# A hybrid S5, retention and ConvGLU layer on one Trainium2 core: S5 state tables for chunks of 16 steps in place of 8, with the side work paced anew

## The chip, the core and the metric

The kernel runs on one core of a Trainium2 chip. The time is the device time of one execution in microseconds (us). A core has five engines with queues of their own: PE (TensorE, matrix products; PEld is its weight load), DVE (VectorE), ACT (ScalarE), POOL (GpSimd) and SP (SyncE, which here issues the transfers). They meet only at semaphores.

## The reference, cut to what matters

```python
hx = modulate(rms_norm(x, norm1_w), mx[0], mx[1])              # 2048 tokens x 1024, 256 context tokens likewise
ux, qx, kx, vx, gx = split_projection(hx @ w_in, rotate=True)  # S5 input u (512), retention q, k, v, g (512 each)
# S5: 32 groups x 16 channels, complex diagonal state of 64, both directions
bu = einsum('gnp,blgp->blgn', b_bar, u);  h[t] = lam_bar * h[t-1] + bu[t]
y  = real(einsum('gpn,blgn->blgp', c_mat, h_f + h_b)) + d * u
s5_x = gelu(y) * sigmoid(gelu(y) @ w_glu + b_glu)
# retention: 4 heads of 128, chunks of 128 tokens, both directions, per-head norm, swish gate
ret_x = retention_mixer(qx, kx, vx, gx, ...)
x = x + mx[2] * (concat([s5_x, ret_x]) @ w_out)
x = x + mx[5] * conv_ffn(modulate(rms_norm(x, norm2_w), mx[3], mx[4]), w_up, conv_w, conv_b, w_down)
return rms_norm(x, final_norm_w)
```
`mx` are the six adaLN vectors, `silu(c) @ w_mod + b_mod`. All data are float32.

## The kernel before, in words

**Stages.** (1) Table stage, 0 to 264 us: adaLN for the first norm, norm and transposition of the tokens in tiles of 256 (`norm_tile`, L563), the S5 input projection (`u_tile`, L615), the S5 tables (`s5_tables`, L422) and the retention's context state. (2) Sweeps, 264 to 897 us. (3) GLU stage, 897 to about 1010 us. (4) Output projection, to 1210. (5) The up half of the FFN, to 2112. (6) The down half, to 2618. Stages 4 to 6 hold no line of the change.

Large products are made of three float32r matmuls (`mm3`, L153 to L156: high by high, high by low, low by high); smaller ones (S5, retention) are plain float32, and the trace shows each of those as two records. Splits into high and low are an ACT copy and a subtraction at L159.

**S5.** The state is not advanced token by token. Tables let one matmul inject 8 tokens of a group into a chunk state (`Dinj`, from JT and JO), one read 8 outputs from the state before a chunk (`Drd`, from GT), and one add what the tokens of a chunk give each other (the Toeplitz table `DT`, from TT). So 2304 tokens (256 context, 2048 latent) are 288 chunks, held as 18 blocks of 16. `s5_tables` makes the tables in 8 groups of four steps: GT (six DVE operations, L433 to L438), TT (PE L450, DVE L456 to L460, a store), JT (six POOL operations, L470 to L475), JO (PE transposes L482, ACT L484, a store L485). One step is taken per round of the norm and projection loop, the rest before the context tile.

**S5 generator** (`s5_gen`). For each of 4 batches of 8 groups: `s5_inj` loads U and the tables and injects (PE L887, ACT L889 to L891 into X); `s5_scan` runs 15 steps within the blocks, all 18 blocks abreast (four DVE operations on 128x288, L904 to L907), then 17 steps over the blocks (four on 128x16, L916 to L919); `s5_fix` carries the block states in (DVE L933 to L939, POOL L932 to L940, on 128x480, 16 rounds in all); `s5_read` copies X to E (ACT L956, L957), multiplies (PE L965 to L967), applies GELU and stores (L970).

**Sweeps.** Sixteen sweeps (two halves of the tokens, four heads, first k and v, then q and g) of eight units; a unit is 24 float32r matmuls of 256 columns, rotary work on DVE (L802, L803), POOL (L804) and copies on ACT. The loop that drives them counts a ninth unit for each k-v sweep, so two sweeps are 17 units and all are 136. Side work is stepped from that loop: the S5 generator at 1.9 steps per unit until it ends; then, after two units, the retention generators (`ret_gen`, one per head, put on a list when the q-g sweep of the second half of their head is done) at two steps per unit; and, from sweep 9, the late modulation (`mod_late`: 16 pieces, each a 1 MB load, eight DVE operations at L685 and L687, one PE matmul L691, three steps a piece). What is left of the retention is stepped four at a time in the rounds of the GLU stage (`glu_gen`).

The instruction order of each engine is made when the program is built, by a scheduler that follows program order, priorities and its own timeline.

## Time and profile before

| what | value |
|---|---|
| median of 3 runs (lowest, highest) | 2618.12 us (2611.74, 2619.86) |
| the profiled execution: its own time, its span | 2620.0 us, 2618.2 us |
| PE, PEld busy | 92%, 78% of the span |
| DVE, ACT, POOL busy | 65%, 39%, 45% |
| mean granted TensorE clock | 0.973 |

The shares are means over six stages with different limits; for this change only the first three count. Busy time of an engine is the time in which at least one of its instructions ran, and an instruction that waits for a port counts as running. PE's ends are modelled, so its work is better counted in matmuls times the distance between their starts.

### The profile page before, as it was taken

The numbers are of one execution on the slowest core, as the hardware profiler recorded it, in microseconds if no ns is written. First come the engines' busy times: TensorE is split into PE (matmuls) and PEld (weight loads), VectorE is DVE, ScalarE is ACT, GpSimd is POOL, SyncE is SP. The second block draws the span as 40 slices with busy tenths as digits, with TensorE's granted clock in tenths as the row PEclk, the third lists the DMA queues.
The fourth block names the chain that finished last, engine by engine and source line by source line (L and its number), as shares of the span: only waits on it lengthen the run. The fifth ranks groups of instructions, "written<-read, shape, count | busy, mean of one in ns | idle before, by whom it ended". The sixth has DMA issues, their size and how long they took to land.

```text
span 2618.2 us, 35766 instructions
## 1 busy us (share of the span) xinstructions
PE 2421.5 (92%) x12896; PEld 2039.7 (78%) x12896; DVE 1700.4 (65%) x3387; ACT 1009.7 (39%) x1697; POOL 1189.6 (45%) x852
## 2 busy tenths in 40 slices
PE   7889987888899978997999999999999999999998
PEld 3779887777898967885788888778888878788876
DVE  9893398998386695667656656756556543636454
ACT  2444746563432442222333333433333332324332
POOL 2354253454334352212677777877777700303120
PEclk9899999999999989999999999999999999999999
DMA  8545633435787653556222222422222264545442
GB/s 251 194 144 144 165 97 108 123 120 177 226 250 246 213 182 123 157 167 198 103 97 73 73 97 73 153 73 75 93 76 75 75 253 145 198 144 197 156 169 89
DMA packets 334319, 377.83 MB, mean 144 GB/s; under 512 B 43942, under 2 KB 284410, under 8 KB 331838
## 3 DMA queue, kind: packets, MB, share of 16 engines
q1 hardware_dynamic: 332702, 374.98, 44.5%
q8 instruction: 102, 1.67, 0.3%
q10 hardware_dynamic: 1440, 0.56, 0.1%
q14 instruction: 75, 0.61, 0.1%
HBM read 268.00 MB, written 107.47 MB: 143 GB/s over the span
## 4 chain that ended last, share of the span: by engine, by line
PE 59%; DVE 20%; DMA 7%; ACT 4%; issue 4%; POOL 3%; SPq 2%; DVEq 0%; ACTq 0%; POOLq 0%
PE mm L1504 17%; PE sc L1504 9%; PE y L1504 4%; PE mm L154 4%; PE mm L155 4%; PE mm L156 4%; PE y L154 2%; PE y L155 2%; PE y L156 2%; POOL w L159 2%; PE sc L154 2%; PE sc L155 2%; PE sc L156 2%; DMA x<-in_x_dram 1%; PE tr L154 1%
## 5 line engine op out<-in xcount | busy, mean ns | idle before, releaser
L159 POOL TENSOR_TENSOR w<-stg,w 128x512 fp32r<-128x512 f32 (+1 forms) x268 | 538.3, 2024 | 214.2 <-ACT w L1440 95.1
L1504 PE MATMUL mm<-hc,w 128*128 128x512 f32 x2112 | 526.1, 397 | 11.3 <-POOL w L159 7.4
L1504 PEld LDWEIGHTS mm<-hc,w 128*128 128x128 f32 x2112 | 398.1, 189 | 111.1 <-POOL w L159 9.2
L1504 PE MATMUL sc<-hc,w 128*128 128x512 f32 x1056 | 278.1, 399 | 2.3 <-POOL w L159 1.4
L159 DVE TENSOR_TENSOR bw<-draw,bw 128x1536 fp32r<-128x1536 f32 x88 | 159.1, 1813 | 183.8 <-ACT bw L1622 183.5
L1504 PEld LDWEIGHTS sc<-hc,w 128*128 128x128 f32 x1056 | 200.3, 190 | 52.4 <-POOL w L159 2.4
L1622 ACT ACTIVATE bw<-draw 128x1536 fp32r<-128x1536 f32 x88 | 130.6, 1487 | 270.5 <-PE tr L156 214.7
L804 POOL TENSOR_TENSOR ob<-ra,rb 128x128 f32<-128x128 f32 x128 | 72.8, 569 | 311.0 <-DVE rb L803 192.6
L154 PE MATMUL mm<-w,hT 128*128 128x256 f32 x688 | 207.5, 302 | 1.9 <-ACT ob L849 1.9
L155 PE MATMUL mm<-w,hT 128*128 128x256 f32 x688 | 204.9, 298 | 0.0
L156 PE MATMUL mm<-w,hT 128*128 128x256 f32 x688 | 204.3, 297 | 0.0
L1649 POOL TENSOR_TENSOR acc<-acc,tm 128x512 f32<-128x512 f32 x24 | 35.1, 1484 | 325.9 <-DVE tm L1648 318.3
L1504 PE MATMUL y<-hc,w 128*128 128x512 f32 x528 | 150.3, 396 | 0.0
L154 PEld LDWEIGHTS mm<-w,hT 128*128 128x128 f32 x688 | 134.6, 196 | 6.6 <-ACT ob L849 2.4
L155 PEld LDWEIGHTS mm<-w,hT 128*128 128x128 f32 x688 | 134.3, 195 | 2.3 <-issue 0.4
L156 PEld LDWEIGHTS mm<-w,hT 128*128 128x128 f32 x688 | 133.8, 194 | 2.1 <-issue 0.4
L1597 DVE TENSOR_TENSOR A<-A,t 128x1024 f32<-128x1024 f32 x44 | 78.3, 1780 | 77.0 <-ACT A L1515 40.8
L1504 PEld LDWEIGHTS y<-hc,w 128*128 128x128 f32 x528 | 99.1, 188 | 24.0
L1429 ACT ACTIVATE w<-stg 128x512 fp32r<-128x512 f32 x44 | 27.8, 633 | 213.5 <-POOL stg L1427 213.5
L155 PE MATMUL y<-w,hT 128*128 128x256 f32 x336 | 102.8, 306 | 0.0
L156 PE MATMUL y<-w,hT 128*128 128x256 f32 x336 | 102.3, 304 | 0.0
L159 POOL TENSOR_TENSOR mh<-mix,mh 128x1024 fp32r<-128x1024 f32 x16 | 38.9, 2431 | 138.9 <-ACT mh L1338 114.4
(464 smaller groups left out, 6397.9 us busy)
## 6 DMA issues: line engine op xcount, KB each, us to landing
stg<-in_w_up_dram SPq DMA_DIRECT2D x44, 1024.0 KB
draw<-in_w_down_dram SPq DMA_DIRECT2D x88, 512.0 KB
stg<-in_w_in_dram SPq DMA_DIRECT2D x44, 512.0 KB
Dact<-A SPq DMA_DIRECT2D x44, 512.0 KB
draw<-Dact SPq DMA_DIRECT2D x88, 256.0 KB
stg<-in_w_mod_dram SPq DMA_DIRECT2D x16, 1024.0 KB
hst<-Dhc SPq DMA_DIRECT2D x10, 1024.0 KB
wm<-in_w_mod_dram SPq DMA_DIRECT2D x8, 1024.0 KB
```

The costliest lines, as they stand in the source:

```text
L154: PE.matmul(ps, lh, rh, start=start, stop=False)
L155: PE.matmul(ps, lh, rl, start=False, stop=False)
L156: PE.matmul(ps, ll, rh, start=False, stop=stop)
L159: eng.tensor_tensor(lo, src, hi.bitcast(F32), op=ALU.subtract)
L804: (GP if 1 else V).tensor_tensor(dst.rearrange("p (i j) -> p i j", j=2), ta, tb, op=ALU.add)
L1429: A.activation(w[:, 0, j], x, AF.Copy)
L1504: PE.matmul(ps, wt[:, wl, j, k], t[:, tl, k], start=start and k == 0 and m == 0, stop=k == 3 and m == 2, skip_group_check=not start)
L1597: V.tensor_tensor(As[j], As[j], T1[j], op=ALU.mult)
L1622: A.activation(w[:, 0], s, AF.Copy)
L1649: (V if g == NG - 1 else GP).tensor_tensor(ac[:, ns], ac[:, ns], tm, op=ALU.add)
```

## The change

A chunk becomes 16 steps. U stays in the old layout of 8 and is read with a step of 2, so each product over a chunk is two matmuls, for the even and the odd half. There are 144 chunks, 9 blocks of 16. The tables GT (10 powers to 18), TT (15 to 31), JT and JO (8 to 16) about double; TT and JO now share one buffer, JO is made and stored in two halves. `s5_fix` takes four groups at a time in two rounds per batch. The late modulation starts with sweep 3, and the retention takes 2.34 steps per unit. The h tiles get 96 bytes more per partition.

```diff
-        return h_pool.tile([P, 2, KT, TS], F32R, tag="hT", name="hT", bufs=4)
+        return h_pool.tile([P, 2 * KT * TS + 24], F32R, tag="hT", name="hT", bufs=4)[:, 0:2 * KT * TS].rearrange("p (l k n) -> p l k n", l=2, k=KT)
...
-    V.tensor_copy(pw[:, 9], pw[:, 8])
+    cmul_pow(pw, 9, 8, 1, 8)
+    V.tensor_copy(pw[:, 17], pw[:, 16])
...
-            GT = s_pool.tile([P, 2, 4, 10, Q], F32, tag="GT", name="GT")
+            GT = s_pool.tile([P, 2, 4, 18, Q], F32, tag="GT", name="GT")
...
-            V.tensor_tensor(GT[:, 1], GT[:, 1], tA, op=ALU.subtract)
+            V.scalar_tensor_tensor(GT[:, 1], GT[:, 1], -1.0, tA, op0=ALU.mult, op1=ALU.subtract)
...
-            TT = s_pool.tile([64, 2, 15, Q], F32, tag="TT", name="TT")
+            TT = s_pool.tile([64, 2, 31, Q], F32, tag="JO", name="TT")
...
-            V.tensor_copy(TT[:, :, 0:7], pv1[:, :, 0:7])
-            V.tensor_copy(TT[:, :, 8:15], pv0[:, :, 1:8])
+            V.tensor_copy(TT[:, :, 0:15], pv1[:, :, 0:15])
+            V.tensor_copy(TT[:, :, 16:31], pv0[:, :, 1:16])
...
-            JT = s_pool.tile([P, 2, 4, T8, Q], F32, tag="JT", name="JT")
+            JT = s_pool.tile([P, 2, 4, T16, Q], F32, tag="JT", name="JT")
...
-            JO = s_pool.tile([P, 4, 2, P], F32, tag="JO", name="JO")
             for g2 in range(2):
-                pj = ps_sc()
+                JO = s_pool.tile([P, 2, 4, P], F32, tag="JO", name="JO")
                 for j in range(2):
+                    pj = ps_sc()
                     for r in range(2):
-                        PE.transpose(pj[:, (2 * j + r) * P:(2 * j + r + 1) * P],
-                                     JT[:, r, 2 * g2 + j].rearrange("p s q -> p (s q)"), ident)
-                A.activation(JO[:, 2 * g2:2 * g2 + 2].rearrange("p g r c -> p (g r c)"), pj, AF.Copy)
-            SP.dma_start(Dinj[b][:, hb * 1024:(hb + 1) * 1024], JO.rearrange("p g r c -> p (g r c)"))
+                        for h in range(2):
+                            PE.transpose(pj[:, (2 * r + h) * P:(2 * r + h + 1) * P],
+                                         JT[:, r, 2 * g2 + j, 8 * h:8 * h + 8].rearrange("p s q -> p (s q)"), ident)
+                    A.activation(JO[:, j].rearrange("p a c -> p (a c)"), pj, AF.Copy)
+                SP.dma_start(Dinj[b][:, (2 * hb + g2) * 1024:(2 * hb + g2 + 1) * 1024], JO.rearrange("p g a c -> p (g a c)"))
...
                 for r in range(2):
-                    ps = next(alt_s) if wide[0] else ps_sc()
-                    PE.matmul(ps[:, 0:NCC], mt[:, gi, r], Us[-1][:, g % 4], start=True, stop=True)
+                    for h in range(2):
+                        PE.matmul(ps[:, r * MCC:(r + 1) * MCC], mt[:, gi, r, h], Uh[:, h], start=(h == 0), stop=(h == 1))
...
+                A.activation(Xg[0:64, :, 0:KB], blk(pv[0:64]), AF.Copy)
+                A.activation(Xg[64:128, :, 0:1], blk(pv[64:128, :, 0:MCX][:, :, ::-1]), AF.Copy)
+                A.activation(Xg[64:128, :, 1:KB], blk(pv[64:128, :, MCX:MCC][:, :, ::-1]), AF.Copy)
...
-            pa = s_pool2.tile([P, GB, 2, 18], F32, tag="fa", name="pa")
+            pa = s_pool2.tile([P, GB, 2, KB], F32, tag="fa", name="pa")
...
-        for k in range(1, 18):
+        for k in range(1, KB):
...
-        for g4 in range(4):
-            go = 2 * g4
+        for g4 in range(2):
+            go = 4 * g4
...
-            M = s_pool2.tile([P, 4, P], F32, tag="M", name="M", bufs=1)
+            M = s_pool2.tile([P, 4, 3, P], F32, tag="M", name="M", bufs=1)
...
-                    PE.matmul(ps[:, 0:NCL], M[:, g], Us[g4][:, g, NCX:NCC], start=True, stop=False)
-                    PE.matmul(ps[:, 0:NCL], rd[:, 0, gi], Ev[:, gi, 0], start=False, stop=False)
-                    PE.matmul(ps[:, 0:NCL], rd[:, 1, gi], Ev[:, gi, 1], start=False, stop=True)
+                    PE.matmul(pv, M[:, g, 1], Uh, start=True, stop=False)
+                    for h in range(2):
+                        PE.matmul(pv[:, h], M[:, g, 2 * h], Uh[:, 1 - h], start=False, stop=False)
+                        PE.matmul(pv[:, h], rd[:, 0, gi, h * P:(h + 1) * P], Ev[:, gi, 0], start=False, stop=False)
+                        PE.matmul(pv[:, h], rd[:, 1, gi, h * P:(h + 1) * P], Ev[:, gi, 1], start=False, stop=h == 1)
...
                 with tc.high_priority(offset=1):
-                    ok = not pend or step(pend[0], 2)
+                    racc += 2.34
+                    n = int(racc)
+                    racc -= n
+                    ok = not pend or step(pend[0], n)
...
-            if i >= 9 and ucount % 1 == 0:
+            if i >= 3:
                 step(ml)
```

## Rows read from the trace of the kernel before

**Rows 1.** Busy time by stage; columns: stretch, length, engines busy, clock, DMA share, GB/s
```profile
64.00:210.00 146.00, 123.82 (x970) 109.15 (x970) 130.53 (x272) 68.68 (x126) 65.98 (x48) 0.94 0.53 164
264.00:345.00 81.00, 75.36 (x521) 69.56 (x520) 41.01 (x111) 57.73 (x144) 20.13 (x23) 0.98 0.54 149
345.00:690.00 345.00, 286.16 (x1886) 262.34 (x1887) 295.78 (x740) 187.48 (x348) 164.80 (x147) 0.95 0.45 131
690.00:897.00 207.00, 194.49 (x1535) 184.32 (x1534) 135.36 (x527) 64.50 (x185) 75.53 (x101) 0.98 0.76 237
897.00:1032.00 135.00, 103.68 (x731) 96.01 (x730) 111.24 (x314) 58.63 (x116) 55.15 (x45) 0.89 0.55 174
```

**Rows 2.** Timeline of PE: start, duration, records; three places
```profile
885.74 0.28 PE L154 MATMUL mm<-w,hT 128*128 128x256 f32 x1
...
886.92 0.28 PE L155 MATMUL mm<-w,hT 128*128 128x256 f32 x1
...
373.68 0.59 PE L967 MATMUL sc<-E,rd 128*128 128x256 f32 x2
374.11 0.59 PE L966 MATMUL tr<-E,rd 128*128 128x256 f32 x2
...
208.02 0.93 PE L482 MATMUL sc<-cst,JT 128*128 128x128 f32 x7
```

**Rows 3.** Groups of instructions, DVE, 0 to 264 us: count | busy, mean ns | idle
```profile
L435 DVE TENSOR_TENSOR GT<-GT,ct 128x640 f32<-128x640 f32 x8 | 6.5, 810 | 0.0
...
L457 DVE COPY TT<-sc 64x224 f32<-64x224 f32 x8 | 3.0, 374 | 0.0
```

**Rows 4.** Groups of instructions, POOL, 64 to 210 us, then 264 to 697 us
```profile
L475 POOL TENSOR_TENSOR JT<-JT,ct 128x512 f32<-128x512 f32 x8 | 11.4, 1430 | 0.6
...
L935 POOL TENSOR_TENSOR X<-X,fb 128x480 f32<-128x480 f32 x16 | 22.6, 1411 | 0.9
```

**Rows 5.** Timeline of DVE while POOL makes one JT: start, duration
```profile
166.97 1.03 DVE L165 TENSOR_SCALAR rsy<-vv 128x2 int32<-128x2 int32 x1
...
168.64 1.02 DVE L173 TENSOR_TENSOR rst<-rsy 128x2 f32<-128x2 f32 x1
...
170.33 1.24 DVE L174 SCALAR_TENSOR_TENSOR rst<-rst,vv 128x2 f32<-128x2 f32 x1
171.60 0.16 DVE L175 SCALAR_TENSOR_TENSOR rsy<-rst,rsy 128x2 f32<-128x2 f32 x1
```

**Rows 6.** Timeline of POOL in the same stretch
```profile
167.93 1.72 POOL L473 TENSOR_TENSOR JT<-PJ,BB 128x512 f32<-128x512 f32 x1
```

**Rows 7.** Groups of instructions, DVE, 264 to 697 us
```profile
L906 DVE TENSOR_TENSOR X<-X,pa 128x288 f32<-128x288 f32 x60 | 37.1, 619 | 0.1
...
L687 DVE SCALAR_TENSOR_TENSOR mac<-stg,sil,mac 128x256 f32<-128x256 f32 x38 | 25.5, 672 | 0.6
L918 DVE TENSOR_TENSOR X<-X,qa 128x16 f32<-128x16 f32 x68 | 19.6, 288 | 0.0
...
L939 DVE TENSOR_TENSOR X<-X,fa 128x480 f32<-128x480 f32 x16 | 18.1, 1133 | 0.3
```

**Rows 8.** Groups of instructions, ACT, 264 to 697 us
```profile
L956 ACT ACTIVATE E<-X 64x1088 f32<-64x1088 f32 x16 | 35.0, 2186 | 8.3 <-PE tr L967 4.5 <-POOL X L940 3.7
...
L889 ACT ACTIVATE X<-tr 64x288 f32<-64x288 f32 x32 | 21.4, 669 | 1.6 <-PE tr L887 1.1
```

**Rows 9.** Groups of instructions, PE, 690 to 897 us
```profile
L155 PE MATMUL mm<-w,hT 128*128 128x256 f32 x349 | 103.1, 295 | 0.0
```

**Rows 10.** The two stores that end the S5 and the GLU: ns, first and last start in us
```profile
L970 SPq DMA_DIRECT2D Dy<-Y x128: 302/422/1327, 376.6 to 696.6; - x128
...
L1234 SPq DMA_DIRECT2D Ds<-so x32: 319/320/627, 907.5 to 1009.9; - x32
```

**Rows 11.** Busy time of the stretch after the last piece of late modulation, columns as in Rows 1
```profile
860.00:890.00 30.00, 30.00 (x255) 29.84 (x254) 12.36 (x56) 9.92 (x26) 12.24 (x17) 1.00 0.54 160
```

**Rows 12.** Instructions of tile mac: ns min/median/max, first and last start in us
```profile
L691 PE MATMUL sc<-mac,cst x32: 377/377/634, 643.5 to 857.1; 128*1 128x256 f32 x32
```

More of the change, by code (lines that the diff above doesn't have):

```diff
@@ L31 @@
 NCC = NCL + NCX
+T16 = 16
+MCL = SEQ // T16
+MCX = CTX // T16
+MCC = MCL + MCX
+KB = MCC // 16
+KP = 10
 GB = 8
@@ L104, in layer_kernel @@
     Du = dram("Du", [512, T8, NCC])
-    DT = dram("DT", [G // 2, 33, 480])
-    Dinj = dram("Dinj", [NB, P, GB * 2 * P])
-    Drd = dram("Drd", [NB, P, 2 * GB * P])
+    DT = dram("DT", [G // 2, 33, 992])
+    Dinj = dram("Dinj", [NB, P, GB * 4 * P])
+    Drd = dram("Drd", [NB, P, 2 * GB * 2 * P])
     Dtab = dram("Dtab", [P, 34 * G])
@@ L228, in load_x @@
         SP.dma_start(XT[t], xsrc[t])
-    lam = s_pool.tile([G, 2, P], F32, name="lam")
-    stp = s_pool.tile([G, 2], F32, name="stp")
+    lams = s_pool.tile([G, 2 * P + 2], F32, tag="ct2", name="lam")
+    lam = lams[:, 0:2 * P].rearrange("g (r n) -> g r n", r=2)
+    stp = lams[:, 2 * P:2 * P + 2]
     for d, nm in enumerate(("f", "b")):
@@ L298, in late_columns @@
         V.tensor_copy(dcol, pt[0:64, 0:8])
-    sw = [s_pool.tile([G, P], F32, name=f"sw{i}") for i in range(6)]
+    sws = s_pool.tile([G, 8, P], F32, tag="JO", name="sw")
+    sw = [sws[:, i] for i in range(6)]
     exp_to(n_pool, stp, stp, G, 2)
@@ L372, in layer_kernel @@
     V.tensor_tensor(BB[:, 1], BB[:, 1], t1v, op=ALU.add)
[L374 to L375 removed]
+    ptab = s_pool.tile([P, 18 * 2 * G + 17 * 2 * G], F32, tag="JT", name="ptab")
+    pw = ptab[:, 0:1152].rearrange("p (e r g) -> p e r g", e=18, r=2)
     V.memset(pw[:, 0, 0], 1.0)
@@ L884, in s5_inj @@
                 g = 2 * g4 + gi
+                ps = next(alt_s) if wide[0] else ps_sc()
+                Uh = Us[-1][:, g % 4].rearrange("p (c h) -> p h c", h=2)
                 for r in range(2):
-                    ps = next(alt_s) if wide[0] else ps_sc()
-                    PE.matmul(ps[:, 0:NCC], mt[:, gi, r], Us[-1][:, g % 4], start=True, stop=True)
-                    Xg = X[:, g, r].rearrange("p (j k) -> p k j", k=18)
-                    A.activation(Xg[0:64], ps[0:64, 0:NCC].rearrange("p (k j) -> p k j", j=16), AF.Copy)
-                    A.activation(Xg[64:128, 0:2], ps[64:128, 0:NCX][:, ::-1].rearrange("p (k j) -> p k j", j=16), AF.Copy)
-                    A.activation(Xg[64:128, 2:18], ps[64:128, NCX:NCC][:, ::-1].rearrange("p (k j) -> p k j", j=16), AF.Copy)
+                    for h in range(2):
+                        PE.matmul(ps[:, r * MCC:(r + 1) * MCC], mt[:, gi, r, h], Uh[:, h], start=(h == 0), stop=(h == 1))
+                pv = ps[:, 0:2 * MCC].rearrange("p (r c) -> p r c", r=2)
+                Xg = X[:, g].rearrange("p r (j k) -> p r k j", k=KP)
+                blk = lambda v: v.rearrange("p r (k j) -> p r k j", j=16)
+                A.activation(Xg[0:64, :, 0:KB], blk(pv[0:64]), AF.Copy)
+                A.activation(Xg[64:128, :, 0:1], blk(pv[64:128, :, 0:MCX][:, :, ::-1]), AF.Copy)
+                A.activation(Xg[64:128, :, 1:KB], blk(pv[64:128, :, MCX:MCC][:, :, ::-1]), AF.Copy)
                 yield
     def s5_scan(b, X, lb):
-        Xk = X.rearrange("p g r (j k) -> p g r k j", k=18)
-        lr = lb[:, :, 0:1].unsqueeze(3).to_broadcast([P, GB, 2, 18])
+        Xk = X.rearrange("p g r (j k) -> p g r k j", k=KP)[:, :, :, 0:KB]
+        lr = lb[:, :, 0:1].unsqueeze(3).to_broadcast([P, GB, 2, KB])
         li = s_pool2.tile([P, GB, 2], F32, tag="li", name="li", bufs=2)
@@ L923, in s5_fix @@
     def s5_fix(b, X, lb, E):
-        Xk = X.rearrange("p g r (j k) -> p g r j k", k=18)
-        for g4 in range(4):
-            go = 2 * g4
-            S = lambda r: Xk[:, go:go + 2, r, 15:16, 1:17].to_broadcast([P, 2, 15, 16])
-            Lp = lambda r: lb[:, go:go + 2, 17 * r:17 * r + 15].unsqueeze(3).to_broadcast([P, 2, 15, 16])
-            o = lambda r: Xk[:, go:go + 2, r, 0:15, 2:18]
-            fa = s_pool2.tile([P, 2, 15, 16], F32, tag="fa", name="fa")
-            fb = s_pool2.tile([P, 2, 15, 16], F32, tag="fb", name="fb")
+        Xk = X.rearrange("p g r (j k) -> p g r j k", k=KP)
+        NK = KB - 1
+        for g4 in range(2):
+            go = 4 * g4
+            sh = [P, 4, 15, NK]
+            S = lambda r: Xk[:, go:go + 4, r, 15:16, 0:NK].to_broadcast(sh)
+            Lp = lambda r: lb[:, go:go + 4, 17 * r:17 * r + 15].unsqueeze(3).to_broadcast(sh)
+            o = lambda r: Xk[:, go:go + 4, r, 0:15, 1:KB]
+            fa = s_pool2.tile(sh, F32, tag="fa", name="fa")
+            fb = s_pool2.tile(sh, F32, tag="fb", name="fb")
             GP.tensor_tensor(fb, Lp(0), S(1), op=ALU.mult)
@@ L1152, in layer_kernel @@
     acc = 0.0
+    racc = 0.0
     ucount = 0
```

85 lines of the change are left out of this document (41 added, 44 removed).

## The prediction, made before the changed kernel ran

> **What bounds the kernel now.** I read the page's slices first, then the busy time by stage, then the groups and timelines inside the stages that the change touches. The busy time by stage [rows 1] shows two stages in which DVE, not PE, is full: the table stage, where DVE is busy for 130.5 of 146 us, and the sweeps that carry the S5 generator, 295.8 of 345 us. Behind them, from 690 to 897 us, PE is the fuller one (194.5 of 207, DVE 135.4), and in the GLU stretch DVE leads again (111.2 of 135 against 103.7).
>
> PE's real work is better counted in matmuls. Ten float32r matmuls of 256 columns start within 1.18 us, so one takes 0.118 and a unit of 24 takes 2.83 us; two float32 records of 256 columns take 0.43 us; the seven transposes of 128 columns, 0.93 us with a 0.27 us tail, stand 0.11 apart [rows 2]. With these, 690 to 897 us holds 349 x 3 matmuls of a sweep [rows 9] (123.5 us), and its other 488 records (42 of state updates and 26 of modulation at 0.215, 420 at 0.11) 61 us: 184 us of work in 207, a share of 0.89. The S5 part, 264 to 690, holds 83 units (235 us), 86 state records (18), 128 injection records of 288 columns (31) and 192 read records (41): 327 of 426 us, a share of 0.77. After the last modulation piece, whose matmul is at 857 [rows 12], PE is full for 30 of 30 us [rows 11].
>
> DVE's busy time contains waiting. While POOL makes one JT, a DVE operation on 128x2 takes 1.02 or 1.24 us, and one of the same kind takes 0.16 us once POOL's operation has ended [rows 5, 6]. In the 4.6 us from 166.97 to 171.60, all covered by POOL, DVE did five operations (two of 0.8 us, three small ones) worth about 2 us: each microsecond of POOL cost DVE about half a microsecond.
>
> **The table stage (loss).** GT: 48 operations go from 640 to 1152 elements. A 640-element operation takes 810 ns [rows 3], an undisturbed 288-element one 0.46, so an element costs 1.0 ns and each operation 0.52 us more: +25 us. TT: 16 copies of 224 elements, 374 ns [rows 3], become 480: 0.26 us each, +4. The larger power tables in the set-up, six products of 256 elements and eight copies longer by 256, less one operation dropped: +4. Together +33 us of DVE's own time. The subtraction turned into a three-operand form I price at nothing, being one operation for one.
>
> JT: 48 POOL operations of 512 elements, 1430 ns in the row [rows 4], become 1024; their shortest in the trace is 1.06 us, so each grows by about 1.0: POOL +48 us. At half a microsecond each DVE is held up 24 us more; the bounds are 0 (POOL works while DVE reads PSUM) and 48. The Trainium skill, "SBUF — State Buffer", section "Who interferes with whom", says that a DVE instruction with two SBUF inputs and a GpSimd instruction that reads SBUF exclude each other for a whole instruction. By that rule alone, at full price, the term would be 48 instead of 24; the rows show half.
>
> DVE has 15.5 us of idle time in the 146 [rows 1]; I let it absorb half, -8. PE gets 64 more transposes (7 us) and twice the columns in L450; ACT gets 16 more JO copies of 0.6 us. Both stay under DVE (PE's share of true work in this stage is about 0.75, ACT's 0.47), so nothing; if DVE were not the limit, some 20 us of PE work would show. TT and the two halves of JO share one buffer: each must wait for the store before it to land, on DVE or on ACT with the norm's copies queued behind. Groups come about 18 us apart and a landing takes some 2.5 us, so three fit: 0, with 20 (8 x 2.5) as the far bound. SP gets eight more stores, and 8 MB more are written while the transfer engines are half free: 0. **Sum: +33 + 24 - 8 = +49 us (25 to 95).**
>
> **The S5 part of the sweeps.** The generator had 168 steps: 12, then 4 x (19 + 8 + 12). It has 12 + 4 x (17 + 4 + 12) = 144. At 1.9 per unit it ends at unit 76, not 89 (its last store is at 696.6 [rows 10]).
>
> DVE: the scan within blocks goes from 288 to 144 elements in 240 operations, four lines of which one is 37.1 us [rows 7]; by 0.46 to 0.31, 143 becomes 96, -47. The steps over blocks fall from 272 to 128 operations, four lines of about 18 us [rows 7]: -37. The carry falls from 64 to 32 operations of the same size [rows 7]: -32. With overlaps I take -110. POOL's half of the carry, 85 us in four lines [rows 4], halves. ACT: E goes from 1088 to 576 elements, 2.2 us to 1.2, in 32 operations [rows 8], and the X copies are half as many, 0.67 us for the largest [rows 8]: about -70 us. Against that all 16 modulation pieces now lie here: each is 8 operations of about 0.5 us and one small addition, 66 us in all, of which 30 were here already (38 of 112 [rows 7]): +36. DVE's load becomes 337 - 110 + 36 = 263 us.
>
> PE: the injection keeps its columns. The read goes from 192 records of 256 columns to 64 of 256 and 384 of 128: 13.8 + 42.2 = 56 us, +15. The odd-even step of the moving operand and the 96 bytes I price at nothing: the distance of 0.118 us is what it would show in, and 1 ns in it is 4 us over both stages, either way. Work for 76 units: 215 + 17 (state) + 31 + 56 + 7 (modulation) = 326 us.
>
> What share does PE reach? 0.77 with DVE 79% busy, 0.89 with DVE 65% busy. At 263 of some 375 us (70%) the line between them gives 0.85; ACT's relief makes me take 0.87: **375 us (bounds 0.83 and 0.95: 393 and 343).**
>
> The added transfers, some 24 MB of tables and modulation weights, lift the transfer engines' share from 0.45 [rows 1] to about 0.67. The 1 MB modulation loads pass on SP in front of S5's small loads and use the same two staging buffers as the sweep weights; hidden as long as the generator is fetched ahead, else a landing of a few us at each of 8 table loads, within the lower bound.
>
> **The rest of the sweeps and the GLU.** Units 77 to 85 have neither generator, since the first retention head comes only with sweep 9: nine units of 3.05 us (with a state update each second one) at 0.93: 30 us. From there 51 units with 51 x 2.34 = 119 steps, of which the three heads on hand use 114: 144 + 10 + 48 chunks of 11 records at 0.11 (58) = 213 us. The modulation is gone here, so I take 0.96, between 0.89 and the full stretch [rows 1, 11]: 222 us. Sweeps: 375 + 30 + 222 = 627 for 633, **-6**.
>
> Left for the GLU: before, 152 steps less 45 x 2 = 62, 15.5 rounds of four; after, 38, 9.5 rounds. A round without retention is 2.83 us of PE, say 3.2; the 17 rounds took 113 us (897 to the last store, 1010 [rows 10]), so one with retention takes 7.0. After: 9.5 x 7.0 + 7.5 x 3.2 = 91, **-22**.
>
> **Sum.** +49 - 6 - 22 = +21 us on the profiled execution's 2620.0 us (span 2618.2): 2641. That execution lies 2 us above the median shown, so I forecast a median of 2639, slower by 0.8%. About 0.3%, 8 us, is what a measurement of this kernel can tell from no change.
>
> **Rivals.** (a) *Faster: PE runs free in the S5 part.* Place: sweeps 0 to 8. If DVE's stalls there were only its own saturation, PE goes at the share of a stage without it, 0.95: 343 us instead of 375, and the total is +49 - 38 - 22 = -11, 2607. It decides at 0.92, where the three terms cancel. For it: PE is full as soon as modulation ends [rows 11], and ACT is relieved. Against it: the modulation that caused those stalls moves into this very part.
> (b) *Slower still: POOL's hold on DVE at its full length.* Place: JT in the table stage, 48 us instead of 24: 2663. The 1.24 us of a 0.16 us operation [rows 5] speaks for it, the five operations that got through against it. The rule of the Trainium skill quoted above ("SBUF — State Buffer") would make it so.
> (c) *No change.* POOL's longer operations fall into DVE's own longer GT operations, which then wait on nothing more: the 24 us do not come, +49 becomes +25: 2615.
> (d) That the change doesn't do what it says would show as a count of 128x288 operations in the scan that has not changed; the diff leaves no room for it.
>
> **Chances.** Forecast 0.32, (a) 0.31, (b) 0.16, (c) 0.21. Hence slower 0.48, same 0.21, faster 0.31. The range holds (a) with its lower half cut at a share of about 0.99 and (b) with a part of the buffer wait: 2590 to 2675. The forecast's own range, by the shares 0.85 and 0.89, is 2631 to 2648.
>
> **What would show it.** The table stage ends (first unit of sweep 0) near 313 us, GT operations take 1.3 us, JT ones 2.0 to 3.0, and small DVE operations beside them up to 2 us. The scan shows 128x144 forms, 0.31 us; the last Dy store comes 375 us after sweep 0 starts; the sweeps end 627 us after their start; the GLU's last store follows 91 us later. It is wrong in its first step if the table stage grows by under 25 us, in its second if PE's share in the S5 part is over 0.92.

## The result, and the profile after

The changed kernel takes **2697.15 us** (median of 4 runs, 2693.54 to 2697.99), the kernel before 2617.38 beside it on the same chip: ratio **1.0305** (95% interval 1.0286 to 1.0324), 80 us slower. The direction was forecast, the size was not: 2639 lay 58 us too low, and the result is 22 us above the range.

Where the 77 us between the two profiled spans (2618.2 and 2695.6) lie follows from a few starts in each trace: of the ACT copies ob, eight to a sweep (the first one opens sweep 0, the 81st sweep 10, the last one ends the sweeps), and of the last Ds5 store, which ends the GLU; "rest" is what lies behind it. "S5 part" is the time from the first unit to the last Dy store, the prediction's 76 units.

| kernel | first unit | sweeps 0 to 9 | sweeps 10 to 15 | GLU | rest | (S5 part) |
|---|---|---|---|---|---|---|
| before | 264.0 | 412.2 | 220.0 | 113.6 | 1608.3 | 432.6 |
| after | 333.3 | 422.2 | 226.4 | 104.0 | 1609.8 | 409.2 |
| difference | +69 | +10 | +6 | -10 | +1 | |
| forecast | +49 | all sweeps -6 | | -22 | 0 | 375 |

So all three terms came out higher than forecast: the table stage by 20 us, the sweeps by 22, the GLU by 12. The busy time by stage of the kernel after (stretch, length, then PE, PEld, DVE, ACT, POOL busy, clock, DMA share, GB/s) answers to [rows 1]:

```profile
64.00:290.00 226.00, 163.32 (x1110) 134.73 (x1109) 195.55 (x289) 81.02 (x150) 116.05 (x48) 0.83 0.48 156
290.00:333.00 43.00, 41.33 (x327) 40.41 (x327) 6.01 (x20) 15.88 (x26) 26.51 (x12) 0.99 0.55 148
333.00:755.00 422.00, 371.85 (x2754) 350.11 (x2752) 260.04 (x770) 174.20 (x385) 143.59 (x133) 0.96 0.70 200
755.00:982.00 227.00, 210.84 (x1692) 207.31 (x1692) 121.75 (x523) 72.82 (x210) 80.44 (x117) 0.95 0.55 175
982.00:1086.00 104.00, 79.25 (x564) 76.45 (x564) 90.08 (x223) 50.87 (x99) 44.98 (x30) 0.84 0.51 164
```

The stage in which DVE is full lasted 146 us (64 to 210, DVE 130.5, idle 15.5 [rows 1]); it now lasts 226 (64 to 290) with DVE 195.6 busy and 30.4 idle. DVE's work grew by 65, its idle time did not shrink but doubled, +15, and the stretch behind it, in which the last projections run nearly without DVE (6 us of it), went from 54 to 43 us, -11. That is the +69. In the sweeps DVE is busy for 260 us, as forecast (263), and is no longer the fuller engine.

The groups of DVE and POOL instructions of the kernel after, 64 to 333 us (count | busy, mean ns | idle), answer to [rows 3, 4]:

```profile
L166 DVE TENSOR_TENSOR hT<-h,hT 128x512 fp32r<-128x512 f32 x29 | 24.1, 843 | 3.1 <-ACT hT L613 3.1
L182 DVE SCALAR_TENSOR_TENSOR rsy<-rst,rsy 128x2 f32<-128x2 f32 x22 | 19.2, 871 | 0.2
...
L441 DVE TENSOR_TENSOR ct<-PR,CT 128x1152 f32<-128x1152 f32 x8 | 12.5, 1561 | 0.0
...
L443 DVE TENSOR_TENSOR GT<-PR,CT 128x1152 f32<-128x1152 f32 x7 | 11.6, 1650 | 0.0
...
L444 DVE TENSOR_TENSOR ct<-PR,CT 128x1152 f32<-128x1152 f32 x8 | 10.7, 1342 | 0.0
...
L464 DVE COPY TT<-sc 64x480 f32<-64x480 f32 x8 | 5.1, 643 | 10.2 <-PE sc L457 10.2
```
```profile
L479 POOL TENSOR_TENSOR JT<-JT,ct 128x1024 f32<-128x1024 f32 x8 | 21.5, 2682 | 0.1
L477 POOL TENSOR_TENSOR JT<-PJ,BB 128x1024 f32<-128x1024 f32 x8 | 20.4, 2549 | 114.5 <-PE sc L490 97.0 <-DVE ltg L427 17.5
L482 POOL TENSOR_TENSOR JT<-JT,ct 128x1024 f32<-128x1024 f32 x8 | 20.0, 2500 | 0.6
```

An undisturbed GT operation takes 1.34 us, a copy 0.64, and JT's six lines have means of 2.2 to 2.7: the sizes of the forecast. What to look at is L182, 22 operations on 128x2 with a mean of 871 ns (the same operation undisturbed: 160). The timelines of DVE and of POOL around 208 us (start, duration) show how that comes:

```profile
207.74 0.84 DVE L180 TENSOR_TENSOR rst<-rsy 128x2 f32<-128x2 f32 x1
208.62 0.16 DVE L181 SCALAR_TENSOR_TENSOR rst<-rst,vv 128x2 f32<-128x2 f32 x1
208.81 2.23 DVE L182 SCALAR_TENSOR_TENSOR rsy<-rst,rsy 128x2 f32<-128x2 f32 x1
211.07 0.16 DVE L180 TENSOR_TENSOR rst<-rsy 128x2 f32<-128x2 f32 x1
```
```profile
206.64 1.93 POOL L481 TENSOR_TENSOR ct<-PJ,BB 128x1024 f32<-128x1024 f32 x1
208.65 2.37 POOL L482 TENSOR_TENSOR JT<-JT,ct 128x1024 f32<-128x1024 f32 x1
211.10 1.93 POOL L478 TENSOR_TENSOR ct<-PJ,BB 128x1024 f32<-128x1024 f32 x1
```

POOL's L482 runs from 208.65 to 211.02. The DVE operation that begins just behind it, at 208.81, ends at 211.04, with POOL's; the next one passes in 0.16 us between two of POOL's. A small operation thus costs DVE what is left of POOL's, and POOL's are now twice as long. One rule of the Trainium skill ("SBUF — State Buffer", section "Who interferes with whom") is that a DVE operation with two SBUF inputs and a GpSimd operation that reads SBUF lock each other out for a whole instruction; this pair agrees with it.

Where DVE idles is seen in the chain of waits of the kernel after, 261 to 284 us (start, duration, what):

```profile
261.02 3.42 DVE GT L443
...
264.93 2.12 DMA DT<-TT
...
267.29 0.60 ACT JO L492
...
267.94 1.98 PE sc L490 x8
...
269.99 2.22 POOL JT L477
272.22 1.88 POOL JT L480
274.10 2.31 POOL JT L479
...
276.48 1.92 POOL ct L481
...
278.49 2.34 POOL JT L482
...
280.87 1.51 PE sc L490 x6
...
283.04 2.62 DMA Dinj<-JO
```

At the end of the stage a group is a bare chain: TT's store must land before the shared buffer can take JO, PE must have read one JT (the transposes) before POOL may write the next, and five of JT's six operations take 11 us, in which DVE has little else left. The busy time of these last 26 us shows it:

```profile
264.00:290.00 26.00, 13.23 (x54) 8.43 (x55) 10.37 (x14) 6.53 (x12) 12.89 (x6) 0.63 0.49 155
```

DVE idles for 15.6 us here, half of its 30.4. PE is busy for only 13.2, and the granted clock is 0.63, so much of the stretch is at the lower of the two levels (1.2 and 2.4 GHz). From 267.9 to 269.9 it is 0.50 throughout: the eight transposes stand 0.21 us apart there, and 0.11 in [rows 2].

### The profile page after: what moved, and what is told of

It reads as the page before. It is cut to its first block, busy times and chain, and to the rows that moved or that the text cites. A ratio compares the mean times of both kernels' runs of the same rounds, so it can differ in the third digit from the quotient of the medians.

```text
span 2695.6 us, 36348 instructions
## 1 busy us (share of the span) xinstructions
PE 2463.3 (91%) x13344; PEld 2084.8 (77%) x13344; DVE 1649.1 (61%) x3216; ACT 949.3 (35%) x1617; POOL 1196.2 (44%) x820
## 4 chain that ended last, share of the span: by engine, by line
PE 57%; DVE 20%; DMA 11%; issue 3%; SPq 3%; POOL 3%; ACT 2%; DVEq 0%; ACTq 0%; POOLq 0%
PE mm L1527 17%; PE sc L1527 8%; PE y L1527 4%; PE mm L162 4%; PE mm L161 4%; PE mm L163 4%; DMA x<-in_x_dram 2%; PE y L161 1%; PE y L163 1%; DVE rsy L182 1%; PE y L162 1%; POOL w L166 1%; PE sc L161 1%; DMA stg<-in_w_mod_dram 1%; PE sc L162 1%
## 5 line engine op out<-in xcount | busy, mean ns | idle before, releaser
L166 POOL TENSOR_TENSOR w<-stg,w 128x512 fp32r<-128x512 f32 (+1 forms) x268 | 534.7, 2012 | 208.0 <-ACT w L1463 95.1
L166 DVE TENSOR_TENSOR bw<-draw,bw 128x1536 fp32r<-128x1536 f32 x88 | 159.7, 1821 | 182.6 <-ACT bw L1645 182.3
L161 PE MATMUL mm<-w,hT 128*128 128x256 f32 x736 | 219.6, 298 | 8.0 <-ACT vz L864 3.7
L163 PE MATMUL mm<-w,hT 128*128 128x256 f32 x736 | 216.8, 295 | 0.0
L162 PE MATMUL mm<-w,hT 128*128 128x256 f32 x736 | 216.0, 293 | 0.0
L161 PEld LDWEIGHTS mm<-w,hT 128*128 128x128 f32 x736 | 142.8, 194 | 12.5 <-ACT vz L864 8.2
L163 PEld LDWEIGHTS mm<-w,hT 128*128 128x128 f32 x736 | 142.7, 194 | 1.7 <-issue 0.9
L162 PEld LDWEIGHTS mm<-w,hT 128*128 128x128 f32 x736 | 143.0, 194 | 1.2 <-issue 0.4
L166 POOL TENSOR_TENSOR mh<-mix,mh 128x1024 fp32r<-128x1024 f32 x16 | 39.0, 2437 | 143.3 <-ACT mh L1361 127.5
L1577 DVE SCALAR_TENSOR_TENSOR t<-G,colp,t 128x1024 f32<-128x1024 f32 x44 | 96.5, 2194 | 1.5
L161 PE MATMUL mm<-hT,w 128*128 128x256 f32 x240 | 73.9, 315 | 15.5 <-DVE ub L641 9.3
```

Source lines behind the costliest of these rows:

```text
L161: PE.matmul(ps, lh, rh, start=start, stop=False)
L162: PE.matmul(ps, lh, rl, start=False, stop=False)
L163: PE.matmul(ps, ll, rh, start=False, stop=stop)
L166: eng.tensor_tensor(lo, src, hi.bitcast(F32), op=ALU.subtract)
L1577: V.scalar_tensor_tensor(t1, Gt[:, 0:HALF], cw(0), t1, op0=ALU.mult, op1=ALU.add)
```

## Experiments

Each run stands beside runs of the kernel before on its chip; these differ by up to 7 us from chip to chip (medians 2613 to 2621), so small differences between runs are read from the ratios and from the stages. First unit, sweeps 0 to 9, 10 to 15 and GLU as above, in us. The expectations call sweeps 0 to 9 "the first 85 units".

| run | kernel, edit | median | ratio (95%) | first unit | 0 to 9 | 10 to 15 | GLU |
|---|---|---|---|---|---|---|---|
| e1 | after, pacing of before | 2668.66 | 1.0202 (1.0169, 1.0236) | 334.0 | 382.3 | 225.9 | 110.2 |
| e2 | after, TT in tA's buffer | 2713.17 | 1.0383 (1.0359, 1.0408) | 343.9 | 421.6 | 225.2 | 107.2 |
| e3 | after, JT for 8 of 16 steps | 2660.91 | 1.0180 (1.0154, 1.0205) | 299.5 | 420.6 | 224.6 | 102.5 |
| e4 | after, no padding | 2695.46 | 1.0311 (1.0283, 1.0338) | 333.4 | 419.7 | 226.6 | 103.9 |
| e5 | after, modulation from sweep 9 | 2673.52 | 1.0206 (1.0188, 1.0223) | 336.3 | 384.8 | 233.6 | 105.7 |
| e6 | after, Newton steps on PSUM | 2697.84 | 1.0296 (1.0276, 1.0316) | 331.1 | 423.8 | 225.7 | 103.9 |
| e7 | before, Newton steps on PSUM | 2609.14 | 0.9970 (0.9957, 0.9982) | 255.3 | 408.0 | 220.6 | 110.7 |
| e8 | before, JT made twice | 2649.92 | 1.0122 (1.0105, 1.0139) | 292.8 | 408.4 | 220.0 | 118.8 |
| e9 | after, whole norm on PSUM | 2698.90 | 1.0303 (1.0289, 1.0317) | 328.2 | 418.3 | 228.7 | 108.9 |
| e10 | before, whole norm on PSUM | 2621.50 | 1.0007 (0.9996, 1.0018) | 266.3 | 410.6 | 219.5 | 115.5 |
| e11 | after, half the multiply-adds | 2686.04 | 1.0249 (1.0233, 1.0265) | 337.3 | 401.1 | 234.1 | 103.7 |
| e12 | after, half the weights | 2696.57 | 1.0295 (1.0279, 1.0310) | 337.0 | 414.6 | 232.2 | 103.9 |
| e13 | before, GT made twice | 2643.73 | 1.0078 (1.0050, 1.0105) | 288.1 | 411.7 | 222.2 | 114.2 |
| e14 | before, pacing of after | 2636.00 | 1.0059 (1.0039, 1.0079) | 264.8 | 441.9 | 208.3 | 110.2 |

**The pacing undone (e1).**

```diff
-                    racc += 2.34
+                    racc += 2.0
-            if i >= 3:
+            if i >= 9:
                 step(ml)
```


> The changed kernel with the old pacing: late modulation from sweep 9, two retention steps per unit. In the changed kernel the first 85 units (sweeps 0 to 9) take 422 us with PE at a share of 0.81, though DVE is busy for only 62% of them. Theory M (the modulation that was moved into the S5 part holds it up): the first 85 units take 395 us or less, the rest of the sweeps and the GLU give back 25 us or more, the total stays within 10 us of the changed kernel's 2697. Theory C (the S5 part is held by its own chains and its small transfers, whatever else is in it): the first 85 units still take 410 us or more, and since the rest then carries the modulation and the GLU stage 24 retention steps more, the total rises by 10 to 25 us.

Sweeps 0 to 9 fall from 422 to 382 us, the GLU and the rest take 6 us more each, and 28 us come back in all. So the first half of theory M came true (395 us or less). Its second half did not: it had the later stages give back 25 us or more and the total stay within 10 us of 2697. Busy time of sweeps 0 to 9 in this run (columns as above):

```profile
334.00:716.00 382.00, 351.71 (x2707) 340.68 (x2706) 211.58 (x650) 174.22 (x387) 131.74 (x133) 0.97 0.66 187
```

DVE has 48 us less to do there than in the kernel after (260.0). Without the moved modulation the S5 on 16 steps gains 30 us in these sweeps against 412 before: that part of the change does what it is for. The modulation costs 40 us where it was put.

**TT out of the shared buffer (e2).**

```diff
-            TT = s_pool.tile([64, 2, 31, Q], F32, tag="JO", name="TT")
+            TT = s_pool.tile([P, 1152], F32, tag="ct1", name="TT", bufs=1)[0:64, 0:992].rearrange("p (g e q) -> p g e q", g=2, e=31)
```


> The changed kernel with TT taken out of the buffer that it shares with JO (it shares DVE's scratch tile instead). Sweep 0 starts at 333 us in the changed kernel, 264 before; ACT waits 28 us in all for TT's stores to land before it may write JO. Theory B (the shared buffer makes each table group one chain of three store landings, and its tail at 264 to 290 is bare): sweep 0 starts 12 to 20 us earlier, total 2677 to 2685. Theory L (DVE's own longer operations and POOL's hold on it make the stage, the buffer waits lie beside them): sweep 0 starts at most 5 us earlier, total 2692 to 2697.

The stage became 11 us longer, which neither theory allowed for. The waits of the kernel after, 64 to 333 us, and of this run, 64 to 344 us (total, times, longest):

```profile
ACT JO L492 <- DMA DT<-TT: 28.3, 4, 8.9
```
```profile
DVE ct L441 <- DMA DT<-TT: 5.7, 3, 2.5
```

ACT's 28.3 us of waiting for TT's stores are gone, and 5.7 us of DVE's are there in their place, since this buffer is tA's. Yet DVE's operations now last 74 us beyond the shortest of their form, 62 in the kernel after, and POOL's 48 products take 137 us in place of 117. So theory B finds no support here: with ACT's waits taken away, the stage got no shorter. A buffer of TT's own was not tried.

**Half of JT (e3).** The second half of the injection table repeats the first.

```diff
-            GP.tensor_tensor(JT[:, 0], pjr, bre, op=ALU.mult)
+            HF = lambda v: v[:, :, 0:8]
+            JR, JI = JT[:, 0, :, 0:8], JT[:, 1, :, 0:8]
+            pjr, pji, bre, bim, tB = HF(pjr), HF(pji), HF(bre), HF(bim), HF(tB)
+            GP.tensor_tensor(JR, pjr, bre, op=ALU.mult)
...
-                                         JT[:, r, 2 * g2 + j, 8 * h:8 * h + 8].rearrange("p s q -> p (s q)"), ident)
+                                         JT[:, r, 2 * g2 + j, 0:8].rearrange("p s q -> p (s q)"), ident)
```


> The changed kernel with JT made for 8 of its 16 steps; the second half of the injection table repeats the first, so that part of the computation is left out. POOL's table work falls from 116 to about 60 us, everything else stays. Theory L: DVE's held-up time in the table stage falls by about 24 us, sweep 0 starts at 305 to 312 us instead of 333, total 2672 to 2678. Theory B: only the tail's JT gets shorter, by 5 to 6 us, sweep 0 starts at 326 to 330, total 2690 to 2694.

The first unit comes 34 us earlier, more than theory L's 21 to 28, and far beyond theory B's 3 to 7. The whole run gains 36 (33 by the ratios). The groups of POOL, 64 to 300 us, in this run:

```profile
L480 POOL TENSOR_TENSOR JT<-PJ,BB 128x512 f32<-128x512 f32 x8 | 13.0, 1624 | 122.2 <-PE sc L493 104.8 <-DVE ltg L427 17.5
L482 POOL TENSOR_TENSOR JT<-JT,ct 128x512 f32<-128x512 f32 x8 | 12.7, 1592 | 0.1
```

POOL's six lines take 70 us instead of 117. If each DVE operation is charged with its time over the shortest one of its form, DVE's excess in the stage is 62 us in the kernel after and 27 in this run: 35 us less, for 47 us less of POOL, and it is what the stage gained.

**No padding (e4).**

```diff
-h_pool.tile([P, 2 * KT * TS + 24], F32R
+h_pool.tile([P, 2 * KT * TS], F32R
```


> The changed kernel without the 96 bytes per h tile. The distance between float32r matmuls of 256 columns is 0.118 us in both kernels. Theory 0: no difference, within 4 us of 2697. Rival: the padding parts addresses that collide, and without it the matmul distance or the splits that write the h tiles get longer: 5 us or more slower.

No stage differs by more than some 3 us, and the ratio is that of the kernel after: theory 0.

**Modulation late, retention paced anew (e5).**

```diff
-            if i >= 3:
+            if i >= 9:
                 step(ml)
```


> The changed kernel with the late modulation back at sweep 9 and the new retention pace (2.34) kept. With both put back the total fell by 28 us: the first 85 units took 382 us for 422, the rest 226 as before, the GLU stage 110 for 104. Theory M (the moved modulation alone costs the 40 us): first 85 units 378 to 386 us; the rest 226 to 236, since it holds modulation and nine chunks of retention more; GLU 104; total 2660 to 2672. Rival (the pace of the retention is what costs): first 85 units 410 us or more, total 2685 or more.

Sweeps 0 to 9 are nearly those of e1 (385 and 382), sweeps 10 to 15 take 7 us more than after, the GLU 2 more: theory M, though the total, 2673.5, lies just above its 2660 to 2672. The interval of the ratio lies inside that of e1. So 2.34 steps a unit instead of 2 move time from the GLU (-4.5 us against e1) to sweeps 10 to 15 (+7.7) and gain nothing that is measured in the total; what the pacing costs is the modulation's place.

**The Newton steps with one operand in PSUM (e6, e7).**

```diff
-        rs = rsqrt(n_pool, vv, 2)
+        rs = rsqrt_ps(n_pool, vv, 2)
+    def rsqrt_ps(pl, v, n):
+        y = pl.tile([P, n], I32, tag=f"rsy{n}", name="rsy", bufs=2)
+        V.tensor_scalar(y, v.bitcast(I32), -0.5, 1597463007.0, op0=ALU.mult, op1=ALU.add)
+        pp = ps_y()
+        t, vp = pp[:, 0:n], pp[:, n:2 * n]
+        V.tensor_scalar(vp, v, -0.5, None, op0=ALU.mult)
+        rs = y.bitcast(F32)
+        for _ in range(3):
+            V.tensor_tensor(t, rs, vp, op=ALU.mult)
+            V.tensor_tensor(t, t, rs, op=ALU.mult)
+            V.scalar_tensor_tensor(rs, t, 1.5, rs, op0=ALU.add, op1=ALU.mult)
```


> The changed kernel with the Newton steps of the norm's reciprocal root (nine operations on 128x2 per tile) rewritten so that each has one operand in PSUM and at most one in SBUF; one operation is added, the computation is the same. Of the 62 us that DVE's operations in the table stage last beyond their shortest, 41 are in these. Theory L (a DVE operation with two SBUF inputs waits for POOL's running JT operation, one with a single SBUF input does not): they take 0.16 us throughout, sweep 0 starts at 298 to 312 us instead of 333, total 2662 to 2678. Rival (something else slows them, or the next two-input operation simply takes over the wait): sweep 0 starts at 325 us or later.

> The same rewriting in the kernel before, where 20 of 38 us of DVE's lengthened time in the table stage are in these operations. Theory L: sweep 0 starts at 246 to 255 us instead of 264, and the total falls by 8 to 17 us below the kernel before. Rival: within 4 us of it.

In the kernel after it gained nothing. The groups of DVE of e6, 64 to 333 us, tell why:

```profile
L166 DVE TENSOR_TENSOR hT<-h,hT 128x512 fp32r<-128x512 f32 x30 | 46.6, 1571 | 3.4 <-ACT hT L626 2.9
...
L194 DVE TENSOR_TENSOR y<-y,rsy 128x2 f32<-128x2 f32 x24 | 3.8, 158 | 0.3
L193 DVE TENSOR_TENSOR y<-rsy,y 128x2 f32<-128x2 f32 x24 | 3.7, 153 | 0.2
L195 DVE SCALAR_TENSOR_TENSOR rsy<-y,rsy 128x2 f32<-128x2 f32 x24 | 3.6, 151 | 0.4
```

The Newton steps did become free of POOL (0.15 us each; three lines of 51 us in the kernel after are 11 here), but the split L166, the next operation with two operands in SBUF, went from 843 to 1571 ns, 24 us to 47. The hold passes on to the next operation that can be held: the rival's second half. In sum DVE's excess fell from 62 us to 48, and the stage gained 2 of these 14. In the kernel before, with JT half as long, DVE's busy time up to the first unit fell by 8 us (199 to 191), and 9 us of the time did go: **e7, 2609.14 us, ratio 0.9970, is faster than both kernels**, by little (0.3%), but with an interval clear of 1.

**JT made twice in the kernel before (e8).** The six POOL operations are issued a second time.

```diff
             GP.tensor_tensor(JT[:, 1], JT[:, 1], tB, op=ALU.add)
+            GP.tensor_tensor(JT[:, 0], pjr, bre, op=ALU.mult)
...
+            GP.tensor_tensor(JT[:, 1], JT[:, 1], tB, op=ALU.add)
```


> The kernel before with the six JT operations of each table group issued twice: 48 POOL operations of 512 elements more, the same result, nothing added on DVE, PE or SP. Theory L, as in the forecast (half of POOL's time is put upon DVE): POOL plus 55 to 65 us, sweep 0 starts 25 to 32 us later (289 to 296). Theory of the full hold: 45 us later or more. Rival (POOL's work lies beside DVE's): under 8 us later.

The first unit comes 29 us later, for some 69 us more of POOL (48 x 1.43 [rows 4]): 0.42 a microsecond here, as theory L had it, against 34 / 47 = 0.72 in e3.

**The whole norm on PSUM (e9, e10).** On top of e6 and e7:

```diff
-                    V.tensor_scalar(h32[:, k], pt[:, kk * TS:(kk + 1) * TS], MSC[k2][:, 1, w, kk:kk + 1], MSC[k2][:, 0, w, kk:kk + 1],
+                    V.tensor_scalar(pt[:, kk * TS:(kk + 1) * TS], pt[:, kk * TS:(kk + 1) * TS], MSC[k2][:, 1, w, kk:kk + 1], MSC[k2][:, 0, w, kk:kk + 1],
...
-            A.activation(hT[:, 0, sl], h32[:, sl], AF.Copy)
-            split_lo(GP if k2 in NLP else V, hT[:, 1, sl], h32[:, sl], hT[:, 0, sl])
+            hp = pt[:, 0:2 * TS].rearrange("p (k n) -> p k n", k=2)
+            A.activation(hT[:, 0, sl], hp, AF.Copy)
+            split_lo(V, hT[:, 1, sl], hp, hT[:, 0, sl])
+            if t >= 5:
+                A.activation(h32[:, sl], hp, AF.Copy)
```


> The changed kernel, in which the norm of the first pass has no DVE operation with two operands in SBUF left: the Newton steps take one operand from PSUM, and the scaled tile stays in PSUM, from where the split is read; four of the nine tiles are copied to SBUF by 16 ACT operations more, for their store. Theory H (the norm's operations are what POOL holds up): DVE's time over the shortest in the table stage falls from 62 us to some 15 to 25, the first unit of sweep 0 comes at 295 to 312 us instead of 333, and the time is 2660 to 2677. Theory C (POOL's six operations stand in the chain of a group themselves, whatever DVE does beside them): the wait goes on to the GT operations or to POOL, the first unit stays at 325 to 335, and the time at 2690 to 2700.

> The kernel before with the same norm. There the Newton steps alone, taken out of POOL's reach, gave 9 us (264 to 255 at the first unit of sweep 0), and the split had taken over 11 us of the hold. Theory H: another 7 to 12 us, 2597 to 2603. Theory C: nothing more, 2606 to 2612.

The first unit of e9 comes at 328, and the time is 2699: both in theory C's ranges. DVE's excess is 42 us instead of 62, and it now sits on GT; the groups of DVE of e9, 64 to 333 us, and of POOL:

```profile
L166 DVE TENSOR_TENSOR hT<-tr,hT 128x512 fp32r<-128x512 f32 x29 | 19.6, 680 | 4.9 <-ACT hT L627 4.7
L456 DVE TENSOR_TENSOR GT<-PR,CT 128x1152 f32<-128x1152 f32 x7 | 18.5, 2645 | 0.0
```
```profile
L495 POOL TENSOR_TENSOR JT<-JT,ct 128x1024 f32<-128x1024 f32 x8 | 24.6, 3076 | 0.6
```

The split is free (680 ns). This GT product went from a mean of 1.65 us to 2.65, this JT operation from 2.50 to 3.08: the two sets of products hold each other up. In sum GT's six lines take 82 us for 68, and JT's 124 for 117. The edit brought a wait of its own, too. The scaled tile keeps its PSUM bank until the split has read it; in e10 DVE waits 16.3 us for transposes where e7 shows 4.0, and e7's gain is given back (2621.50, outside both theories' ranges). So the pair separates the two theories only in part.

**Half the multiply-adds, half the weights (e11, e12).** Both leave out part of the modulation's sum.

```diff
-        for k in range(1, KT):
+        for k in range(1, 4):
             V.scalar_tensor_tensor(ac, sv[:, k], sil[:, 0, k:k + 1], ac, op0=ALU.mult, op1=ALU.add)
```
```diff
-        SP.dma_start(sv, dap(I["w_mod"], col, [[6144, P], [P * 6144, KT], [1, 256]]))
+        SP.dma_start(sv[:, 0:4], dap(I["w_mod"], col, [[6144, P], [P * 6144, 4], [1, 256]]))
-            V.scalar_tensor_tensor(ac, sv[:, k], sil[:, 0, k:k + 1], ac, op0=ALU.mult, op1=ALU.add)
+            V.scalar_tensor_tensor(ac, sv[:, k % 4], sil[:, 0, k:k + 1], ac, op0=ALU.mult, op1=ALU.add)
```


> The changed kernel with four of the eight multiply-adds of each modulation piece left out (the weights are loaded as before): 64 DVE operations of about 0.48 us fewer in sweeps 3 to 9. The moved modulation costs 40 us there. Theory V (DVE's time is what it costs): 14 to 24 us come back, 2673 to 2683. Theory D (the 1 MB loads and the staging buffers cost it): 0 to 5, 2691 to 2699.

> The changed kernel with half of the modulation weights loaded (four of eight row blocks, used twice, so 0.5 MB a piece instead of 1 MB) and all eight multiply-adds. Theory D: 14 to 24 us come back, 2673 to 2683. Theory V: 0 to 5, 2691 to 2699. If both this and the run with half the multiply-adds give some 10 us, each is half the cost; if neither gives over 5, the cost is the order of the steps in PE's queue, not their length.

In sweeps 0 to 9, half of the multiply-adds takes back 21 of the 40 us, half of the weights 8. Busy time of these sweeps, first of e11, then of e12:

```profile
337.00:738.00 401.00, 361.24 (x2735) 342.33 (x2734) 229.43 (x706) 174.08 (x385) 133.80 (x132) 0.96 0.72 206
```
```profile
337.00:752.00 415.00, 369.31 (x2739) 349.68 (x2739) 267.06 (x768) 175.49 (x388) 136.60 (x133) 0.95 0.64 180
```

DVE's time is the larger part of the cost: 31 us of it less bring 21 us, while 8 MB less of weights (transfer share 0.64 instead of 0.70) bring 8. Both lose 6 to 8 us again in sweeps 10 to 15, as e5 did, and 4 in the table stage, where nothing was changed. So the median of the whole run falls by 11 us and by less than 1 (by the ratios 15 and 3): e12 is in theory V's range, e11 between the two. Theory V holds for sweeps 0 to 9, with the loads as a smaller part; why the later sweeps then grow was not tried.

**GT made twice in the kernel before (e13).** The six DVE operations are issued a second time.

```diff
+            V.tensor_tensor(GT[:, 0], prr, cre, op=ALU.mult)
...
+            V.tensor_tensor(GT[:, 1], GT[:, 1], tA, op=ALU.subtract)
```


> The kernel before with the six DVE operations that make GT issued twice: 48 operations of 0.81 us more, 39 us of DVE's own time in the table stage, nothing else changed. Theory S (DVE's own time counts there at full length, as the prediction took it): the first unit of sweep 0 comes 33 to 45 us later, and the time is 2650 to 2663. Theory K (POOL's products set the pace of the stage and DVE's own time is partly absorbed): 10 to 25 us later, 2628 to 2643.

The first unit comes 24 us later for 39 us of DVE's own work: DVE's own time is paid at 0.62, in theory K's range for the stage (the median, 2643.73, lies just above the one for the time). The run shows one thing more: POOL's 48 products, which are the same, take 92 us in place of 67. The hold works in both directions.

**The new pacing alone (e14).**

```diff
-                    ok = not pend or step(pend[0], 2)
+                    racc += 2.34
+                    n = int(racc)
+                    racc -= n
+                    ok = not pend or step(pend[0], n)
-            if i >= 9 and ucount % 1 == 0:
+            if i >= 3:
```


> The kernel before with the new pacing alone: modulation pieces from the fourth sweep, 2.34 retention steps a unit, S5 on 8 steps as it was. Theory V (the modulation costs its DVE time, whatever S5 does beside it; DVE is 80% busy there): the first 85 units take 35 to 60 us more, the GLU 10 to 20 less, and the time is 2632 to 2660. Theory D (it costs only beside the longer tables' transfers): the first 85 units take 0 to 15 us more, and the time is 2600 to 2618.

Sweeps 0 to 9 take 30 us more, sweeps 10 to 15 12 less, the GLU 3 less: 15 us slower. The modulation costs nearly as much beside the old S5 tables as beside the new ones (30 and 40), so theory D is out; theory V's lower bounds, 35 in the sweeps and 10 in the GLU, were both too high.

## Why the prediction was right in direction and wrong in size

The sign was right for the main reason given, the loss in the table stage; the sweeps, though, were forecast to gain 6 us and lost 16. The size failed in two steps, one in the table stage and one in the sweeps, and in the price of the GLU's rounds.

**The table stage, +69 for +49.** The two terms of DVE's busy time came as worked out. GT at 1.34 us and copies at 0.64 make 30 of the +33; the excess over the shortest operation of each form went from 38 to 62 us, and +24 was the forecast for POOL's hold. The step that failed is "DVE has 15.5 us of idle time in the 146; I let it absorb half, -8". The idle time grew by 15 instead, and 15.6 of the 30.4 us lie in the last 26 us of the stage. The premise of the TT/JO term did not hold either, "groups come about 18 us apart and a landing takes some 2.5 us, so three fit: 0": groups now stand some 27 us apart (GT's first product of successive groups starts at 161.7, 189.3, 216.4 and 242.6 in the chain; the last one, at 259.2, after 17), landings and JT stand in the chain of a group, and ACT's JO copies waited 28.3 us for TT's stores. Whether these waits cost anything is open: e2, without ACT's, has the longer stage.

Priced by runs, the stage splits otherwise than by busy time. JT's doubling is worth 34 us (e3) and not 24. The other 35 are little more than DVE's own +33, if that counts in full; at the price of e13 it is worth 33 x 0.62 = 20 (an estimate), and some 15 us are left. They are as many as the idle time that came in, which e3 keeps (192.0 - 159.1 = 33 us, from 64 to 256 us). Their cause stays open: the landings in the chain and PE's lower clock are candidates, and no run took away one of them alone.

**Rival (b)** priced the hold at 48: e3 gives 34 of it, between the forecast's half and the whole. For one pair of operations the rule of the Trainium skill quoted with it holds (2.23 us for 0.16); for the stage it gives too much. DVE has other operations that pass: h (L607, L599 before), which reads PSUM, has a mean of 531 ns after and 533 before. **Rival (c)** fell with the first unit at 333.

**The S5 part, 409 us for 375.** DVE's load was right (258 us for 263), and so were its parts: the scan's 240 operations on 128x144 take 94 us for 96. Groups of DVE of the kernel after, 333 to 755 us:

```profile
L695 DVE SCALAR_TENSOR_TENSOR mac<-stg,sil,mac 128x256 f32<-128x256 f32 x112 | 55.5, 497 | 1.2
L917 DVE TENSOR_TENSOR pb<-X,li 128x144 f32<-128x144 f32 x60 | 26.1, 435 | 1.5 <-ACT X L903 1.5
...
L918 DVE TENSOR_TENSOR X<-X,pa 128x144 f32<-128x144 f32 x60 | 19.4, 324 | 0.0
...
L693 DVE TENSOR_SCALAR mac<-stg,sil 128x256 f32<-128x256 f32 x16 | 5.6, 352 | 21.0 <-DMA stg<-in_w_mod_dram 20.9
```

The step that failed is PE's share, "0.77 with DVE 79% busy, 0.89 with DVE 65% busy", "the line between them gives 0.85; ACT's relief makes me take 0.87". By the prediction's own count of 326 us of work it was 326 / 409 = 0.80, under its lower bound, though DVE was busy for only 258 / 409 = 63% of the time, where the same line gives 0.91. So DVE's busy share alone does not set PE's. Without the moved modulation the share is what was forecast: e1's last Dy store comes 362 us after the first unit, and less 14 pieces of two records at 0.215 us (6.0) the work is 320: 0.88.

So the modulation was priced as load (+36 us of DVE's time, 7 of PE's 326) and cost 40 us. Part of how is seen in the waits. PE, in sweeps 0 to 9 of the kernel after:

```profile
PE sc L699 <- DVE mac L695: 5.2, 2, 4.6
...
PE sc L699 <- ACT Y L987: 4.6, 3, 3.5
```

PE's idle time there is 20 us longer than in e1 (422.0 - 371.9 against 382.0 - 351.7), and 10.7 of it stand before the pieces' own matmuls (L699; 0.7 in e1): a matmul that waits for its multiply-adds, or for a GELU copy (Y), holds up what stands behind it in PE's queue. The last line of the groups above adds DVE's waits for the weights, 20.9 us in eight waits; the prediction called these loads "hidden as long as the generator is fetched ahead". The longest wait of ACT, its ob copies behind DVE's rotation (L811), is not the modulation's: 124 us here and 121 in e1. e11 and e12 show the order of the two parts: operations first, loads second. The way of the rest of the 40 us is not shown.

**Rival (a)**, PE free in the S5 part, fell as the forecast did: even without the modulation, in e1, the share was 0.88 and not 0.95.

**The rest of the sweeps** came out 13 us below the forecast (last Dy store to the last ob copy, 239 us for 30 + 222), and that is luck. The prediction counts 76 + 9 + 51 = 136 units at 24 matmuls; the ninth unit of each k-v sweep holds none of these, and 128 units do: 8 x 2.83 = 23 us of work that does not exist. It falls to this part. The prediction has 60 units here; the trace has 1180 matmuls of sweeps behind the last Dy store (49 units) and 1864 before it (78). Counted rightly, the work behind it is 139 + 10 + 59 = 208 us, 0.87 of the 239, where the forecast took 0.93 and 0.96. Without the miscount the forecast for all sweeps would have been some 24 us lower still.

**The GLU, -10 for -22.** The count was right: 16 of the 64 retention chunks are left for it, 25 before (the prediction's 38 and 62 steps of 152 make 16 and 26). The price was wrong: nine chunks less gave 9.6 us, 1.1 each, where the prediction had 22 / 9 = 2.5. It divided the whole 113 us by rounds, though not all of that time goes by rounds: after the change the first retention copy of the stretch comes 8 us after its start. e1 and e14, with 20 chunks each, both take 110.2. Runs of one pacing differ by up to 8 us here (before, e7, e8, e10, e13: 110.7 to 118.8, mean 114.6; after and its like: 102.5 to 108.9, mean 104.9), and their means are 9.7 apart.

**Priced at nothing, and rightly:** the 96 bytes (e4).
